# The low-weight blocks of a split fp32 weight tile at a pitch of 160 columns instead of 128

## The chip, the cores and the metric

The kernel runs on one core of one Trainium2 chip. Its time is the time on the device in microseconds (us), and the figure compared is the median over several executions. Engine names are those of the profile: PE is the matrix engine, PEld its weight loads (they overlap PE), DVE is VectorE, ACT is ScalarE, POOL is GpSimd, SP is the engine whose queue issues most DMAs.

## The reference

Two layers of a bidirectional hybrid encoder over 272 rows (16 learned meta tokens and 256 tokens) of width 2048, in float32:

```
proj = h @ w_in                              # 2048 x 6176
y_gla = gla_mixer(q, k, v, r, low-rank decay)
y_na  = na_mixer(q, k, v, rel_bias)
h  = layer_norm(ALPHA * h + concat(y_gla, y_na) @ w_out)
ff = square(relu(h @ w_ff1)) @ w_ff2         # 2048 -> 8192 -> 2048
h  = layer_norm(ALPHA * h + ff)
```

The meta tokens are dropped from the output. Nearly all the arithmetic is in the four products with `w_in`, `w_out`, `w_ff1` and `w_ff2`; the change touches how the weights of these products lie in the on-chip memory (SBUF), and nothing else.

## The kernel before, in words

**Split products.** A float32 weight `w` is split into a high part `wh` (the value rounded to the matrix engine's format `float32r`) and a low part `wl = w - wh`. Activations are split in the same way into a pair (high, low). A product is the sum of three: `wh` with the high activations, `wh` with the low ones, `wl` with the high ones.

**Weight tiles.** Weights stream from HBM in tiles of 128 partitions x 1024 columns (`WB`), 512 KB each, 768 of them in all, in the fixed order of `order` (line 150). `made` (line 172) issues a tile's DMA on SP's queue into `raw`, lets ACT copy it into `wh` (line 180) and DVE subtract into `wl` (line 181). `raw`, `wh` and `wl` come from the pool `wst` with three buffers for each name, so a new `wh` is written when the matmuls of the tile three places earlier have been done. `weights` (line 166) keeps two tiles made ahead. The very first tile goes through `head` (line 186), in quarters.

**Blocks.** Each tile holds eight blocks of 128 x 128, the stationary operands of eight matmuls. In `wh` and `wl` a block begins 128 columns (512 bytes) behind the one before it, so that all blocks begin at a multiple of 512 bytes from the tile's start.

**Three orders of matmuls.** `eight` (line 204), called by `by_m` (line 250), uses a tile for one output of 128 columns. In layer 0 (272 rows, now and then 274) it issues for each of eight blocks one matmul with the high and one with the low activations (line 216, 16 in all, high and low in turn), and then eight with `wl` and the high activations (line 219). In layer 1 most products need 256 rows alone; then high and low activations lie side by side, one matmul of 512 columns does both (line 213, eight in all), and eight of 256 columns with `wl` follow (line 219). `by_k` (line 230) uses a tile for four outputs in four PSUM banks: it issues its matmuls (line 246) in groups of four outputs, four with the high activations, four with the low ones, and so on, those with `wl` last.

**Activations.** A pair lies in one tile of two rows of 288 columns (`PITCH`, line 40): the low part of 272 columns begins 288 columns, that is 1152 bytes or 4.5 x 256, behind the high one. A `dense` pair of layer 1 (line 43) has its low part 256 columns, or 1024 bytes, behind the high one. `PAD` (line 39) is a dummy tile ahead of everything else that shifts where the later tiles begin. With a scratch area of 8192 bytes at the start of each partition, the tiles `x`, `y`, `u` of the activations, `raw`, `wh` and `wl` all begin at a multiple of 256 bytes.

The call that makes the program (line 1175) sets aside that scratch area (`dynamic_dma_scratch_size`).

Of the kernel before, what the change touches and what calls it, by code (L numbers as in the profile page):

```python
# [7 lines left out]
F32 = mybir.dt.float32  # L8
F32R = mybir.dt.float32r
U8 = mybir.dt.uint8  # L10
AF = mybir.ActivationFunctionType
ALU = mybir.AluOpType
PSUM = bass.MemoryType.PSUM

P = 128
# [11 lines left out]
WB = 1024  # L27
# [10 lines left out]
MEET = 2  # L38
PAD = 40
PITCH = 288  # L40


class Pair(tuple):
# [10 lines left out]
class Trunk:  # L54
# [117 lines left out]
    def made(self, ap, ends):  # L172
        if ap is None:
            return None
        nc = self.nc
        raw, wh, wl = (self.wp.tile([P, WB], d, name=nm, tag=nm)
                       for nm, d in (("raw", F32), ("wh", F32R), ("wl", F32R)))
        for c in map(slice, (0,) + ends, ends):
            nc.sync.dma_start(raw[:, c], ap[:, c])
            nc.scalar.copy(wh[:, c], raw[:, c])  # L180
            self.wl = nc.vector.tensor_tensor(wl[:, c], raw[:, c], wh[:, c].bitcast(F32), ALU.subtract).ins  # L181
        if not ends:
            self.head(ap, raw, wh, wl)
        return wh, wl

    def head(self, ap, raw, wh, wl):

        nc, q = self.nc, WB // 4
        both = self.xr.tile([P, 2, q + L], F32, name="head", tag="head", bufs=1)
        self.x[:2] = [self.pair(self.xp, "x", c) for c in range(2)]  # L190
        for c in range(2):
            nc.sync.dma_start(both[:, c], self.i["head"][:, c])
        nc.sync.dma_start(raw[:, 2 * q:], ap[:, 2 * q:])
        for c in range(2):
            at = slice(c * q, c * q + q)
            h, lo = (t[:, :L] for t in self.x[c])
            todo = [(both[:, c, q:], h, lo), (both[:, c, :q], wh[:, at], wl[:, at])]
            for args in todo[::-1] if c else todo:
                self.split(*args)
        for at in (slice(2 * q, 3 * q), slice(3 * q, WB)):  # L200
            nc.scalar.copy(wh[:, at], raw[:, at])
            self.wl = nc.vector.tensor_tensor(wl[:, at], raw[:, at], wh[:, at].bitcast(F32), ALU.subtract).ins

    def eight(self, ps, wh, wl, x, n, first, last, once):

        mm = self.nc.tensor.matmul
        c = lambda w, j: w[:, j * P:j * P + P]  # L210
        for j, v in enumerate(x):
            if once:
                mm(ps, lhsT=c(wh, j), rhs=v.once, start=first and not j, stop=False)  # L213
                continue
            for i in range(2):
                mm(ps[:, :n], lhsT=c(wh, j), rhs=v[i][:, :n], start=first and not i + j, stop=False)  # L216
        o = ps[:, T:] if once else ps[:, :n]
        for j, (h, _) in enumerate(x):
            mm(o, lhsT=c(wl, j), rhs=h[:, :T if once else n], start=False, stop=last and j == 7)  # L219
# [10 lines left out]
    def by_k(self, acts, n, before, wide=False):  # L230

        ps = [self.pm.tile([P, 512], F32, name="mm", tag="mm") for _ in range(4)]
        if wide:
            ps += [self.bank() for _ in range(4)]
        nk = len(acts)
        for k in range(0, nk, 2):
            before(k)
            for g in range(0, len(ps), 4):
                wh, wl = self.weights()
                parts = ((wh, 0), (wh, 1), (wl, 0))  # L240
                order = [(j, p, m) for j in range(2) for p in range(3) for m in range(4)]
                by_output = k == nk - 2 or k == 0 and not wide
                order.sort(key=lambda o: (o[0], o[2] // 2) if wide and not k + g else (by_output and o[2], o[1] // 2))
                for j, p, m in order:
                    c = j * 512 + m * P
                    self.nc.tensor.matmul(ps[g + m][:, :n], lhsT=parts[p][0][:, c:c + P], rhs=acts[k + j][parts[p][1]][:, :n],  # L246
                                          start=k + j + p == 0, stop=k == nk - 2 and j + p == 3)
        return [p[:, :n] for p in ps]

# [27 lines left out]
    def pair(self, pool, name, c):  # L277
        both = pool.tile([P, 2, PITCH], F32R, name=f"{name}{c}", tag=f"{name}{c}", bufs=1)
        return Pair(both, dense=name in ("y", "u") and not self.full)
# [94 lines left out]
    def load_gates(self):  # L374

        place = lambda c: self.yp.tile([P, 2, PITCH], F32, name=f"gw{c}", tag=f"y{c}", bufs=1).rearrange("p a c -> p (a c)")[:, :512]
        *self.wup, self.wlr = (place(c) for c in (8, 9, 10))
# [563 lines left out]
    def reuse(self, name, c, dtype):  # L941

        t = self.xp.tile([P, 2, PITCH], dtype, name=f"{name}{c}", tag=f"x{c}", bufs=1)
        return t.rearrange("p a c -> p (a c)")[:, :512]
# [235 lines left out]
```

## Time and profile before

| | |
|---|---|
| median of 3 executions | 2366.12 us (2366.05 to 2366.2) |
| the profiled execution | 2366.29 us |
| its span, first to last instruction | 2364.5 us |
| PE busy | 2356.2 us, 18180 matmuls |
| DVE busy | 1520.8 us |
| ACT busy | 1219.3 us |
| DMA | 419.02 MB, mean 177 GB/s |

A matmul's duration in the profile holds its latency, and matmuls overlap: some 287 ns for one of 272 columns, while the next one starts about 125 ns later. What the matrix engine needs for one is therefore read as the distance between starts, in the timeline: the start of a group of like matmuls, the start of the next group, and the count between them. The timeline rounds to 0.01 us, so that eight matmuls give a mean to about 1 ns and sixteen to about 0.6 ns. The line number behind an instruction names the source line, `out<-in` its tiles.

### The profile page before, as it was taken

The numbers are of one execution on the slowest core, as the hardware profiler recorded it, in microseconds if no ns is written. First come the engines' busy times: TensorE is split into PE (matmuls) and PEld (weight loads), VectorE is DVE, ScalarE is ACT, GpSimd is POOL, SyncE is SP. The second block draws the span as 40 slices with busy tenths as digits, with TensorE's granted clock in tenths as the row PEclk, the third lists the DMA queues.
The fourth block names the chain that finished last, engine by engine and source line by source line (L and its number), as shares of the span: only waits on it lengthen the run. The fifth ranks groups of instructions, "written<-read, shape, count | busy, mean of one in ns | idle before, by whom it ended". The sixth has DMA issues, their size and how long they took to land.

```text
span 2364.5 us, 44607 instructions
## 1 busy us (share of the span) xinstructions
PE 2356.2 (100%) x18180; PEld 2241.9 (95%) x18180; DVE 1520.8 (64%) x2432; ACT 1219.3 (52%) x2100; POOL 136.2 (6%) x200
## 2 busy tenths in 40 slices
PE   9999999999999999999999999999999999999998
PEld 9999999999999999999999899999988888888888
DVE  5588777775544455546576787778766455666654
ACT  5666664564433344444456666655644333444443
POOL 0021100100000000000030111101100000000000
PEclk9999999999999999999999999999999999999999
DMA  7454445555555555555555555455566666556664
GB/s 261 153 160 153 156 135 176 173 176 178 177 178 176 176 177 179 177 177 174 177 184 171 164 160 165 155 160 188 187 192 190 189 187 188 188 190 212 195 188 144
DMA packets 118301, 419.02 MB, mean 177 GB/s; under 512 B 13512, under 2 KB 14024, under 8 KB 118096
## 3 DMA queue, kind: packets, MB, share of 16 engines
q1 hardware_dynamic: 117808, 415.65, 55.8%
q8 instruction: 142, 2.33, 0.4%
q14 instruction: 63, 0.52, 0.1%
q10 hardware_dynamic: 288, 0.52, 0.1%
HBM read 414.03 MB, written 2.10 MB: 176 GB/s over the span
## 4 chain that ended last, share of the span: by engine, by line
PE 98%; DVE 1%; issue 0%; ACT 0%; POOL 0%; DVEq 0%; ACTq 0%; POOLq 0%
PE mm L216 35%; PE mm L219 29%; PE mm L213 22%; PE mm L246 6%; PE bg L246 1%; PE bg L757 1%; PE mm L696 1%; PE bg L557 0%; PE bg L403 0%; DVE wl L181 0%; PE mm L722 0%; PE mm L446 0%; PE bg L883 0%; PE bg L608 0%; PE bg L638 0%
## 5 line engine op out<-in xcount | busy, mean ns | idle before, releaser
L181 DVE TENSOR_TENSOR wl<-raw,wh 128x1024 fp32r<-128x1024 f32 (+1 forms) x768 | 941.8, 1227 | 621.5 <-ACT wh L180 618.4
L180 ACT CAST wh<-raw 128x1024 fp32r<-128x1024 f32 (+1 forms) x768 | 803.5, 1047 | 919.4 <-PE mm L216 367.7
L216 PE MATMUL mm<-x,wh 128*128 128x272 f32 (+2 forms) x4224 | 569.8, 287 | 0.0
L216 PEld LDWEIGHTS mm<-x,wh 128*128 128x128 f32 x4224 | 541.1, 188 | 0.8 <-PE mm L696 0.2
L219 PE MATMUL mm<-x,wl 128*128 128x272 f32 (+3 forms) x3264 | 466.9, 285 | 0.0
L219 PEld LDWEIGHTS mm<-x,wl 128*128 128x128 f32 x3264 | 437.5, 189 | 11.6
L213 PE MATMUL mm<-x,wh 128*128 128x512 f32 x1152 | 290.1, 394 | 0.0
L213 PEld LDWEIGHTS mm<-x,wh 128*128 128x128 f32 x1152 | 207.2, 189 | 37.9 <-PE mm L696 0.4
L219 PE MATMUL mm<-y,wl 128*128 128x272 f32 (+1 forms) x1408 | 200.5, 285 | 0.0
L219 PEld LDWEIGHTS mm<-y,wl 128*128 128x128 f32 x1408 | 189.5, 189 | 6.5
L216 PE MATMUL mm<-y,wh 128*128 128x272 f32 (+1 forms) x1440 | 193.3, 286 | 0.0
L216 PEld LDWEIGHTS mm<-y,wh 128*128 128x128 f32 x1440 | 184.3, 188 | 0.0
L213 PE MATMUL mm<-y,wh 128*128 128x512 f32 x688 | 172.6, 392 | 0.0
L219 PE MATMUL mm<-u,wl 128*128 128x272 f32 (+1 forms) x1024 | 145.8, 285 | 0.0
L213 PEld LDWEIGHTS mm<-y,wh 128*128 128x128 f32 x688 | 123.6, 189 | 21.9
L219 PEld LDWEIGHTS mm<-u,wl 128*128 128x128 f32 x1024 | 137.8, 189 | 4.8
L216 PE MATMUL mm<-u,wh 128*128 128x272 f32 (+1 forms) x1056 | 141.2, 286 | 0.0
L216 PEld LDWEIGHTS mm<-u,wh 128*128 128x128 f32 x1056 | 134.9, 188 | 0.0
L213 PE MATMUL mm<-u,wh 128*128 128x512 f32 x496 | 124.2, 392 | 0.0
L213 PEld LDWEIGHTS mm<-u,wh 128*128 128x128 f32 x496 | 89.2, 189 | 15.9
L246 PE MATMUL mm<-x,wh 128*128 128x272 f32 (+1 forms) x512 | 73.3, 288 | 0.0
L246 PEld LDWEIGHTS mm<-x,wh 128*128 128x128 f32 x512 | 67.9, 191 | 0.0
(273 smaller groups left out, 1856.5 us busy)
## 6 DMA issues: line engine op xcount, KB each, us to landing
raw<-in_wff SPq DMA_DIRECT2D x512, 512.0 KB, 3.6
raw<-in_win SPq DMA_DIRECT2D x190, 512.0 KB, 3.8
raw<-in_wout SPq DMA_DIRECT2D x64, 512.0 KB, 3.6
nb<-in_nab SPq DMA_DIRECT2D x16, 352.0 KB, 4.7
xraw<-in_xT SPq DMA_DIRECT2D x7, 272.0 KB, 5.2
out<-out SPq DMA_DIRECT2D x5, 256.0 KB, 3.2
brow<-in_norm SPq DMA_DIRECT2D x4, 256.0 KB, 4.8
gw<-in_wup SPq DMA_DIRECT2D x4, 196.0 KB
```

The costliest lines, as they stand in the source:

```text
L180: nc.scalar.copy(wh[:, c], raw[:, c])
L181: self.wl = nc.vector.tensor_tensor(wl[:, c], raw[:, c], wh[:, c].bitcast(F32), ALU.subtract).ins
L213: mm(ps, lhsT=c(wh, j), rhs=v.once, start=first and not j, stop=False)
L216: mm(ps[:, :n], lhsT=c(wh, j), rhs=v[i][:, :n], start=first and not i + j, stop=False)
L219: mm(o, lhsT=c(wl, j), rhs=h[:, :T if once else n], start=False, stop=last and j == 7)
L246: self.nc.tensor.matmul(ps[g + m][:, :n], lhsT=parts[p][0][:, c:c + P], rhs=acts[k + j][parts[p][1]][:, :n], start=k + j + p == 0, stop=k ...
L696: nc.tensor.matmul(ps[hh][:, t * NKEY:t * NKEY + NKEY], lhsT=q[hs, NM + t * P:NM + t * P + P], rhs=k[hs, t, :], start=True, stop=True)
L757: nc.tensor.matmul(po[t][hs, :P], lhsT=v2[ts, hs] if rest else v1[:, t, hs], rhs=p2[ts, hh, :] if rest else p1[:, 2 * hh + t, :], start=re ...
```

## The change

The high weights stay at a pitch of 128 columns. The low weights' tile grows from 1024 to 1280 columns (`SPAN`), and its blocks begin 128 + 32 (`SKEW`) columns, or 640 bytes, apart: block 0 at a multiple of 256 bytes, block 1 at 128 bytes past one, block 2 at a multiple again. `made`, `head` and the matmuls address blocks in place of columns; count, order, sizes and data of the copies, subtractions and matmuls stay. DVE now writes eight pieces of 128 columns with gaps of 32. The three buffers of `wl` take 3 x 1024 bytes more of each partition, and the scratch area shrinks from 8192 to 2048 bytes.

```diff
+SKEW = 32
+SPAN = 1280
...
-        raw, wh, wl = (self.wp.tile([P, WB], d, name=nm, tag=nm)
-                       for nm, d in (("raw", F32), ("wh", F32R), ("wl", F32R)))
+        raw = self.wp.tile([P, WB], F32, name="raw", tag="raw")
+        blocks = raw.rearrange("p (b c) -> p b c", c=P)
+        wh, wl = self.skewed("wh", 0, WB), self.skewed("wl", SKEW, SPAN)
         for c in map(slice, (0,) + ends, ends):
             nc.sync.dma_start(raw[:, c], ap[:, c])
-            nc.scalar.copy(wh[:, c], raw[:, c])
-            self.wl = nc.vector.tensor_tensor(wl[:, c], raw[:, c], wh[:, c].bitcast(F32), ALU.subtract).ins
+            self.halves(blocks, wh, wl, slice(c.start // P, c.stop // P))
...
+    def skewed(self, name, skew, size):
+        flat = self.wp.tile([P, size], F32R, name=name, tag=name)
+        return bass.AP(flat.tensor, flat.offset, [flat.ap[0], [P + skew, WB // P], [1, P]])
+
+    def halves(self, raw, wh, wl, at):
+        self.nc.scalar.copy(wh[:, at], raw[:, at])
+        self.wl = self.nc.vector.tensor_tensor(wl[:, at], raw[:, at], wh[:, at].bitcast(F32), ALU.subtract).ins
...
-        c = lambda w, j: w[:, j * P:j * P + P]
+        c = lambda w, j: w[:, j]
...
-                    c = j * 512 + m * P
-                    self.nc.tensor.matmul(ps[g + m][:, :n], lhsT=parts[p][0][:, c:c + P], rhs=acts[k + j][parts[p][1]][:, :n],
+                    self.nc.tensor.matmul(ps[g + m][:, :n], lhsT=parts[p][0][:, 4 * j + m], rhs=acts[k + j][parts[p][1]][:, :n],
...
-    nc = bacc.Bacc("TRN2", target_bir_lowering=False, num_devices=1, dynamic_dma_scratch_size=8192)
+    nc = bacc.Bacc("TRN2", target_bir_lowering=False, num_devices=1, dynamic_dma_scratch_size=2048)
```

More of the change, by code (lines that the diff above doesn't have):

```diff
@@ L175, in made, with head @@
         nc = self.nc
-        raw, wh, wl = (self.wp.tile([P, WB], d, name=nm, tag=nm)
-                       for nm, d in (("raw", F32), ("wh", F32R), ("wl", F32R)))
+        raw = self.wp.tile([P, WB], F32, name="raw", tag="raw")
+        blocks = raw.rearrange("p (b c) -> p b c", c=P)
+        wh, wl = self.skewed("wh", 0, WB), self.skewed("wl", SKEW, SPAN)
         for c in map(slice, (0,) + ends, ends):
             nc.sync.dma_start(raw[:, c], ap[:, c])
-            nc.scalar.copy(wh[:, c], raw[:, c])
-            self.wl = nc.vector.tensor_tensor(wl[:, c], raw[:, c], wh[:, c].bitcast(F32), ALU.subtract).ins
+            self.halves(blocks, wh, wl, slice(c.start // P, c.stop // P))
         if not ends:
-            self.head(ap, raw, wh, wl)
+            self.head(ap, raw, blocks, wh, wl)
         return wh, wl
-    def head(self, ap, raw, wh, wl):
+    def skewed(self, name, skew, size):
[4 more added lines that the diff above has]
+        self.wl = self.nc.vector.tensor_tensor(wl[:, at], raw[:, at], wh[:, at].bitcast(F32), ALU.subtract).ins
+    def head(self, ap, raw, blocks, wh, wl):
         nc, q = self.nc, WB // 4
@@ L194, in head @@
         for c in range(2):
-            at = slice(c * q, c * q + q)
+            at = slice(2 * c, 2 * c + 2)
             h, lo = (t[:, :L] for t in self.x[c])
-            todo = [(both[:, c, q:], h, lo), (both[:, c, :q], wh[:, at], wl[:, at])]
+            todo = [(both[:, c, q:], h, lo), (both[:, c, :q].rearrange("p (b c) -> p b c", c=P), wh[:, at], wl[:, at])]
             for args in todo[::-1] if c else todo:
                 self.split(*args)
-        for at in (slice(2 * q, 3 * q), slice(3 * q, WB)):
-            nc.scalar.copy(wh[:, at], raw[:, at])
-            self.wl = nc.vector.tensor_tensor(wl[:, at], raw[:, at], wh[:, at].bitcast(F32), ALU.subtract).ins
+        for at in (slice(4, 6), slice(6, 8)):
+            self.halves(blocks, wh, wl, at)
     def eight(self, ps, wh, wl, x, n, first, last, once):
         mm = self.nc.tensor.matmul
-        c = lambda w, j: w[:, j * P:j * P + P]
+        c = lambda w, j: w[:, j]
         for j, v in enumerate(x):
```

## The prediction

> **What bounds the kernel now.** I read the busy rows and the chain of waits first.
>
> ```profile
> span 2364.5 us, 44607 instructions
> PE 2356.2 (100%) x18180; PEld 2241.9 (95%) x18180; DVE 1520.8 (64%) x2432; ACT 1219.3 (52%) x2100; POOL 136.2 (6%) x200
> ...
> PE 98%; DVE 1%; issue 0%; ACT 0%; POOL 0%; DVEq 0%; ACTq 0%; POOLq 0%
> ```
>
> PE is busy all through, and 98% of the chain that ended last lies on it. So nothing but the distance between the starts of matmuls matters. I took it from the timeline of PE, first in layer 0:
>
> ```profile
> 601.21 2.14 PE L216 MATMUL mm<-x,wh 128*128 128x272 f32 x16
> 603.19 1.16 PE L219 MATMUL mm<-x,wl 128*128 128x272 f32 x8
> 604.19 2.14 PE L216 MATMUL mm<-x,wh 128*128 128x272 f32 x16
> ```
>
> The sixteen matmuls with high weights go from 601.21 to 603.19: 1.98/16 = 123.75 ns each. The eight with low weights go from 603.19 to 604.19: 1.00/8 = 125 ns each, although both have 272 columns. What differs: at line 216 the moving operand begins in turn at a multiple of 256 bytes (high activations) and 128 bytes past one (low), while the weights always begin at a multiple; at line 219 both always begin at a multiple. Narrow windows over the eight show where they lose it:
>
> ```profile
> 603.31 1.04 PE L219 MATMUL mm<-x,wl 128*128 128x272 f32 x7
> 603.45 0.91 PE L219 MATMUL mm<-x,wl 128*128 128x272 f32 x6
> 603.57 0.78 PE L219 MATMUL mm<-x,wl 128*128 128x272 f32 x5
> ```
>
> The steps from the group's start are 0.12, 0.14 and 0.12 us, then 0.62/5 = 0.124 us up to 604.19. The long step stands just where the turn of addresses stops. A second look at the same thing is `by_k` in layer 0, where the same kinds of weight and activation meet in another order, four high ones, then four low ones:
>
> ```profile
> 20.40 2.18 PE L246 MATMUL bg<-x,wh 128*128 128x272 f32 x16
> 22.41 1.17 PE L246 MATMUL bg<-x,wl 128*128 128x272 f32 x8
> 23.42 2.18 PE L246 MATMUL mm<-x,wh 128*128 128x272 f32 x16
> ```
>
> Here the sixteen take 2.01 us, 125.6 ns each, and the eight with low weights 1.01 us, 126 ns each. So sixteen high-weight matmuls of one shape cost 1.98 us where the address changes at each step and 2.01 us where it stays for four. `by_k` also changes the PSUM bank at each step, so the row alone doesn't prove that the address is the cause; that is why "no effect" stays a rival below. Then layer 1:
>
> ```profile
> 1899.97 1.12 PE L219 MATMUL mm<-u,wl 128*128 128x256 f32 x8
> 1900.08 1.00 PE L219 MATMUL mm<-u,wl 128*128 128x256 f32 x7
> 1900.92 2.00 PE L213 MATMUL mm<-u,wh 128*128 128x512 f32 x8
> 1902.08 0.84 PE L213 MATMUL mm<-u,wh 128*128 128x512 f32 x3
> 1902.76 1.12 PE L219 MATMUL mm<-u,wl 128*128 128x256 f32 x8
> ```
>
> The first low-weight matmul takes 0.11 us, the seven others 0.84/7 = 120 ns. Of the eight with 512 columns behind them, the first five take (1902.08 - 1900.92)/5 = 232 ns and the last three 0.68/3 = 227 ns: the change from one kind to the other leaves a trace for some five matmuls. The weight loads differ as well, in two windows of the grouped lines, 400 to 1200 us (layer 0) and 1600 to 2300 us (layer 1):
>
> ```profile
> L219 PEld LDWEIGHTS mm<-u,wl 128*128 128x128 f32 x496 | 66.0, 188 | 0.0
> ...
> L219 PEld LDWEIGHTS mm<-u,wl 128*128 128x128 f32 x432 | 58.9, 190 | 4.2
> ```
>
> A low-weight load takes 188 ns beside moving operands of 272 columns and 190 ns beside those of 256.
>
> **The change part by part.** What the skew can reach is counted by these rows, of the page and of the view by tile:
>
> ```profile
> L219 PE MATMUL mm<-x,wl 128*128 128x272 f32 (+3 forms) x3264 | 466.9, 285 | 0.0
> L219 PE MATMUL mm<-y,wl 128*128 128x272 f32 (+1 forms) x1408 | 200.5, 285 | 0.0
> L219 PE MATMUL mm<-u,wl 128*128 128x272 f32 (+1 forms) x1024 | 145.8, 285 | 0.0
> ...
> L246 PE MATMUL mm<-x,wl x256: 283/286/428, 5.5 to 1702.5; 128*128 128x272 f32 x96, 128*128 128x256 f32 x32
> L246 PE MATMUL mm<-y,wl x128: 279/284/296, 346.5 to 1564.9; 128*128 128x272 f32 x64, 128*128 128x256 f32 x64
> L246 PE MATMUL bg<-x,wl x64: 284/288/291, 10.3 to 53.4; 128*128 128x272 f32 x64
> ...
> L219 PE MATMUL mm<-x,wl 128*128 128x256 f32 x1152 | 160.4, 282 | 0.0
> L219 PE MATMUL mm<-y,wl 128*128 128x256 f32 x704 | 98.2, 282 | 0.0
> L219 PE MATMUL mm<-u,wl 128*128 128x256 f32 x512 | 71.4, 282 | 0.0
> ```
>
> In all 3264 + 1408 + 1024 + 256 + 128 + 64 = 6144 low-weight matmuls, eight for each of 768 tiles; 2368 of them are layer 1's of 256 columns at line 219. Every second one gets its weights from the other half of a 256-byte line.
>
> *Low weights in layer 0 (and `by_k`).* No row shows a weight load at a skewed address here. I take it that what counts is where weights and moving operand begin against each other; then a skewed weight against a straight activation is what a straight weight against a skewed activation is at line 216, and the low-weight group should run at that group's 123.75 ns instead of 125: -1.25 ns. From above it is bounded by nothing gained, and beyond that by the long step: 0.14 against 0.124 us, rounded about +10 ns, at each skewed block. From below by the 0.12 us of the first step: -5 ns.
>
> *Low weights in layer 1.* With 256 columns no row has addresses in turn. The nearest one is again layer 0's, so I take -1.25 ns, with the bounds 113 ns (the first of the group, 0.11 us, seven less than 120) and +10 ns as above.
>
> Together 6144 x 1.25 = 7.7 us less.
>
> *What it leaves behind.* The first five high-weight matmuls after a low-weight group in layer 1 take 232 - 227 = 5 ns more than the last three. There are 2368/8 = 296 such groups; if the new order left nothing behind this would give 296 x 5 x 5 = 7.4 us, if it left twice as much it would cost as much. No row says which: 0.
>
> *DVE's and ACT's share.* DVE writes eight pieces instead of one row; ACT reads and writes the same bytes. The nearest rows are a DVE operation of 272 elements with steps and one without:
>
> ```profile
> L543 DVE TENSOR_TENSOR S<-S,dec 128x272 f32<-128x272 f32 x64 | 27.1, 449 | 0.8 <-ACT U L534 0.5
> L801 DVE TENSOR_TENSOR ft<-ft 128x272 f32<-128x272 f32 x56 | 24.3, 436 | 0.3 <-ACT ft L800 0.3
> ...
> 639.95 2.14 PE L216 MATMUL mm<-y,wh 128*128 128x272 f32 x16
> 642.17 1.05 ACT L180 CAST wh<-raw 128x1024 fp32r<-128x1024 f32 x1 [1.90 <-PE mm L216]
> 643.25 1.23 DVE L181 TENSOR_TENSOR wl<-raw,wh 128x1024 fp32r<-128x1024 f32 x1 [1.72 <-ACT wh L180]
> ```
>
> 449 against 436 is 3%, or 37 ns of 1.23 us; below, nothing. It costs nothing: ACT's copy at 642.17 waited for line 216's matmuls begun at 639.95 to free a buffer, and this tile is used three tiles (of 604.19 - 601.21 = 2.98 us) later, its low part from 639.95 + 8.94 + 1.98 = 650.87. DVE is done at 644.48, over 6 us ahead. With that cover gone it would be 768 x 37 ns = 28 us.
>
> *Scratch area and later tiles.* The issues of DMAs are all by SP and ACT, on two queues beside those of instruction loading; no row shows POOL issuing one:
>
> ```profile
> q1 hardware_dynamic: 117808, 415.65, 55.8%
> q10 hardware_dynamic: 288, 0.52, 0.1%
> ...
> out<-out ACTq DMA_DIRECT2D x2, 256.0 KB, 2.6
> ```
>
> No wait is added, so I set the smaller scratch at 0. Tiles ahead of the low weights move down by 6144 bytes, those behind by 3072; both are multiples of 256, so no other operand changes its half.
>
> **Sum.** The profiled execution took 2366.29 us (its span and 1.8 us around it); 2366.29 - 7.7 = 2358.6. It lies 0.2 us above the median of the runs, so the forecast for the median is 2358.4 us, 0.33% less.
>
> **The rivals.** *No effect.* Order or PSUM bank, not the weights' address, makes 123.75, 125 and 125.6 ns different. For it: the steps of PE are uneven in every order. Then the time stays at 2366.1 +- 1.
>
> The Trainium skill speaks for this rival: "TensorE: Matmul & The Clock Gate", section "Step-by-step: what each phase is for", says that PE reads weights and moving operand through two independent ports, and that loading the next weights takes nothing from the running matmul; by it the sum would be 0. Its section "Back-to-back issue gap" gives N/2.4 + 2.5 ns for an undisturbed matmul, as an estimate 115.8 ns for 272 columns; the 125 ns above do not agree, so that something stalls each step which that page does not name.
>
> *A larger gain.* In layer 1 the weight load itself sets the 120 ns, being held up where it begins in the same half as the moving operand: loads take 190 ns there. If four of eight then take 113 ns, 296 x 4 x 7 = 8.3 us go, with the 7.4 us left behind also gone, and layer 0's and `by_k`'s share 3776 x 1.25 = 4.7: 2366.1 - 20.4 = 2345.7. Against it: the gain of 113 ns is seen once a group, right behind a matmul of 512 columns, which gives the load more time.
>
> *Slower.* In layer 1 the matmul is so short that the load has no slack, and a weight that begins in the other half than the one before makes a long step like that of layer 0, +10 ns, at each of 296 x 4 = 1184 skewed blocks: +11.8 us, less 4.7 in the rest: 2366.1 + 7.1 = 2373.2. It decides from 4.7/1184 = 4 ns a block. For it: the long step of layer 0 stands at a change in the addresses' order. Against it: at line 216 the order changes at every step and that is the fastest group. If layer 0 had the long steps too, with (6144 - 2368)/2 = 1888 skewed blocks, it would be 2366.1 + 11.8 + 18.9 = 2396.8.
>
> **How the numbers follow.** A measurement of this kernel can tell about 0.2% (4.7 us) from no change. The forecast, 2352 to 2362, gets 0.42; the larger gain 0.11; no effect 0.22; slower 0.25, of it 0.05 for long steps in both layers. Faster by over 0.2% (below 2361.4): 0.11 and most of 0.42, the rest of it lying within 0.2%: 0.50. Same 0.25, slower 0.25. The range leaves out the far ends of both sides: 2346 to 2378.
>
> **What would show it.** Right: the low-weight group at line 219 in layer 0 goes from 1.00 to 0.99 us or less, with no step of 0.14, in layer 1 from 0.95 to about 0.94, and line 216 stays at 1.98. The larger gain: in layer 1 0.93 or less and all eight matmuls of 512 columns near 227 ns. No effect: 1.00 and 0.95 stay. Slower: steps of 0.13 us or more at every second low-weight matmul. The forecast is wrong if line 213 or 216, whose operands don't move, changes by more than the low-weight groups, if PE waits for `wl`, or if line 181 takes over 1.5 us.

## The result, and the profile after

The changed kernel takes 2374.39 us (median of 7 executions, 2374.18 to 2375.0) against 2366.37 us before (7 executions beside it): 1.0034 times as long, 95% interval 1.0022 to 1.0046. It is slower by 8 us; 2358.4 us had been forecast.

The page of the changed kernel, busy rows and the chain of waits:

```profile
span 2373.1 us, 44607 instructions
PE 2365.0 (100%) x18180; PEld 2247.9 (95%) x18180; DVE 1520.3 (64%) x2432; ACT 1220.5 (51%) x2100; POOL 135.9 (6%) x200
...
PE 98%; DVE 1%; issue 0%; ACT 0%; POOL 0%; DVEq 0%; ACTq 0%; POOLq 0%
```

As many instructions as before, PE still on 98% of the chain, and the span 8.6 us longer. Line 225 is now the high-weight matmul of layer 0 (216 before), 222 that of layer 1 (213), 228 the low-weight one (219), 254 that of `by_k` (246). The timeline of PE in layer 0, and narrow windows over one low-weight group:

```profile
601.82 2.17 PE L225 MATMUL mm<-x,wh 128*128 128x272 f32 x16
603.82 1.16 PE L228 MATMUL mm<-x,wl 128*128 128x272 f32 x8
604.82 2.17 PE L225 MATMUL mm<-x,wh 128*128 128x272 f32 x16
606.83 1.16 PE L228 MATMUL mm<-x,wl 128*128 128x272 f32 x8
...
603.95 1.04 PE L228 MATMUL mm<-x,wl 128*128 128x272 f32 x7
604.07 0.91 PE L228 MATMUL mm<-x,wl 128*128 128x272 f32 x6
604.20 0.79 PE L228 MATMUL mm<-x,wl 128*128 128x272 f32 x5
...
605.83 1.16 PE L225 MATMUL mm<-x,wh 128*128 128x272 f32 x8
```

The low-weight group still takes 1.00 us. Its long step of 0.14 is gone, its steps are 0.13, 0.12, 0.13 and then 0.62/5, so that nothing is won. The sixteen high-weight matmuls, none of whose operands was moved to another half of its 256 bytes, take 2.00 and 2.01 us instead of 1.98. That isn't a bump at their start: their last eight, from 605.83 to 606.83, take 125 ns each, where the group before had 123.75. The starts of single matmuls, in nanoseconds, show two patterns. Before, the high-weight steps alternate between 126 and 121 ns in 329 of the 373 tiles of 272 columns that no other matmul interrupts; after, they do so in 22, and nearly all others run through four steps of about 125, 128, 124 and 123 ns.

The same in layer 1:

```profile
1900.88 1.11 PE L228 MATMUL mm<-u,wl 128*128 128x256 f32 x8
1901.82 1.99 PE L222 MATMUL mm<-y,wh 128*128 128x512 f32 x8
1903.65 1.10 PE L228 MATMUL mm<-y,wl 128*128 128x256 f32 x8
1904.59 2.03 PE L222 MATMUL mm<-y,wh 128*128 128x512 f32 x8
1906.45 1.11 PE L228 MATMUL mm<-y,wl 128*128 128x256 f32 x8
1907.40 1.76 PE L222 MATMUL mm<-u,wh 128*128 128x512 f32 x7
```

Here the low-weight group went from 0.95 to 0.94 or 0.95 us, and two kinds of tile take turns: 2.77 us (1901.82 to 1904.59) and 2.81 us (1904.59 to 1907.40), although both run the same instructions at addresses of the same halves. Summed over the whole trace, each matmul counted from its start to the start of the next:

| matmuls | before | after | change | forecast |
|---|---|---|---|---|
| high weights, 272 columns, 6016 | 747.8 us | 755.7 | +7.9 | 0 |
| high weights, 512 columns, 2336 | 539.1 | 540.9 | +1.8 | 0 |
| low weights, 272 columns, 3008 | 378.0 | 378.7 | +0.7 | -3.8 |
| low weights, 256 columns, 2368 | 283.0 | 280.4 | -2.7 | -3.0 |
| low weights in `by_k`, 448 | 55.7 | 56.1 | +0.4 | -0.6 |

These make +8.1 of the span's +8.6 us. The loss lies in the matmuls whose own operands the change left alone.

### The profile page after: what moved, and what is told of

It is laid out like the page before. It is cut to its first block, busy times and chain, and to the rows that moved or that the text cites. A ratio compares the mean times of both kernels' runs of the same rounds, so it can differ in the third digit from the quotient of the medians.

```text
span 2373.1 us, 44607 instructions
## 1 busy us (share of the span) xinstructions
PE 2365.0 (100%) x18180; PEld 2247.9 (95%) x18180; DVE 1520.3 (64%) x2432; ACT 1220.5 (51%) x2100; POOL 135.9 (6%) x200
## 4 chain that ended last, share of the span: by engine, by line
PE 98%; DVE 1%; issue 0%; ACT 0%; POOL 0%; DVEq 0%; ACTq 0%; POOLq 0%
PE mm L225 36%; PE mm L228 29%; PE mm L222 22%; PE mm L254 6%; PE bg L254 1%; PE bg L765 1%; PE mm L704 1%; PE bg L565 0%; PE bg L411 0%; DVE wl L194 0%; PE mm L730 0%; PE mm L454 0%; PE bg L891 0%; PE bg L616 0%; PE bg L646 0%
```

## The experiments

Three theories at first. **A**: what counts is where PE reads the low-weight blocks, and the state in which this leaves PE's two streams (weight loads and moving operand) is handed on to the high-weight matmuls behind. **B**: the other tiles' new places in SBUF do it. **C**: DVE's writes with gaps disturb PE's reads.

**All but the skew (e1_layout).**

```diff
-        wh, wl = self.skewed("wh", 0, WB), self.skewed("wl", SKEW, SPAN)
+        wh, wl = self.skewed("wh", 0, WB), self.skewed("wl", 0, SPAN)
```

> All of the change but the skew: the larger tile, the smaller scratch area, block-wise addressing, but low-weight blocks at a pitch of 128 columns again. Theory A (what counts is where the matrix engine reads the low-weight blocks, and the order in which their addresses alternate is handed on to the high-weight matmuls behind them): back to 2366.4 us within 1 us, sixteen high-weight matmuls of layer 0 in 1.98 us. Theory B (the other tiles' new places in SBUF are the cause): stays at 2374 us, sixteen in 2.00 to 2.01 us. Theory C (VectorE's writes with gaps disturb the matrix engine's reads): 2366.4 us, as A.

2366.52 us, 1.0001 of before (0.9991 to 1.001). Its timeline of layer 0:

```profile
702.68 2.14 PE L225 MATMUL mm<-u,wh 128*128 128x272 f32 x16
704.66 1.16 PE L228 MATMUL mm<-u,wl 128*128 128x272 f32 x8
705.66 2.14 PE L225 MATMUL mm<-u,wh 128*128 128x272 f32 x16
```

1.98 and 1.00 us, as before. B falls: the smaller scratch area, the larger tiles and the moved neighbours cost nothing.

**Skewed writes, straight or skewed reads (e2_even, e3_odd).**

```diff
-            mm(o, lhsT=c(wl, j), rhs=h[:, :T if once else n], ...
+            mm(o, lhsT=c(wl, j // 2 * 2), rhs=h[:, :T if once else n], ...      # e2_even
+            mm(o, lhsT=c(wl, j // 2 * 2 + 1), rhs=h[:, :T if once else n], ...  # e3_odd
```

> The changed kernel, low weights still written with gaps, but the low-weight matmuls read only the even blocks (0, 0, 2, 2, 4, 4, 6, 6), which all begin at a multiple of 256 bytes; the odd blocks' part of the products is left out. Theory A: 2366.4 us within 1.5, sixteen high-weight matmuls of layer 0 in 1.98 us. Theory B and theory C: 2374 us.

> As the run that reads even blocks, but only odd blocks (1, 1, 3, 3, 5, 5, 7, 7), all 128 bytes past a multiple of 256; the even blocks' part of the products is left out. Theory A: the relation to the straight activations is constant again, so the low-weight matmuls behave as with even blocks, 125 ns each in layer 0, but what they hand on can differ: between 2360 and 2376 us, and if the time differs from the even run's, at least half of the difference lies in the high-weight matmuls. Theories B and C: 2374 us.

2367.77 us with even blocks, 2377.21 us with odd ones. First the timeline of the even run, then of the odd one:

```profile
701.24 2.14 PE L225 MATMUL mm<-y,wh 128*128 128x272 f32 x16
703.22 1.16 PE L228 MATMUL mm<-y,wl 128*128 128x272 f32 x8
704.22 2.14 PE L225 MATMUL mm<-u,wh 128*128 128x272 f32 x16
```

```profile
702.71 2.17 PE L225 MATMUL mm<-y,wh 128*128 128x272 f32 x16
704.71 1.17 PE L228 MATMUL mm<-y,wl 128*128 128x272 f32 x8
705.72 2.15 PE L225 MATMUL mm<-u,wh 128*128 128x272 f32 x16
707.71 0.54 PE L228 MATMUL mm<-u,wl 128*128 128x272 f32 x3
```

DVE writes with gaps in both. With even blocks the steps are those of the kernel before (1.98 and 1.00), so C falls. It stands 1.5 us above the 2366.26 us of the kernel before beside it. By the starts of all matmuls these lie in `by_k`, which the edit leaves reading skewed blocks: 1.7 us more there, and every other group of matmuls that use weight tiles within 0.1 us. With odd blocks the high-weight group takes 2.00 and 1.99 us and the low-weight one 1.01. By the starts of all matmuls the odd run loses 5.8 us at line 225 and 0.9 at line 222 against the even one, 6.7 of the 9.4 us between the two. The low-weight matmuls of line 228 lose 4.6 us, where they had been expected to stay, and `by_k` takes 1.8 us less. Only the blocks that line 228 reads differ between these two kernels, so where the low weights are read sets the time, and most of the cost is paid by the others: that is theory A. Each of the two kernels ran once; the 17 executions of the kernel before beside them lie within 1.9 us.

**The skewed blocks first (e4_swap).**

```diff
-        for j, (h, _) in enumerate(x):
+        for i in range(8):
+            j = i ^ 1
```

> The changed kernel with all its parts, but the low-weight matmuls take the blocks in the order 1, 0, 3, 2, 5, 4, 7, 6: as many skewed blocks, the last one now a straight one. Theory A: the low-weight group itself stays within 0.01 us, and the high-weight matmuls behind it fall into another pattern: sixteen in layer 0 back at 1.98 us, the whole 2366 us or less. Theories B and C: 2374 us.

2372.38 us, 1.0025 of before (1.0015 to 1.0036). A row of each layer's two groups:

```profile
701.72 2.14 PE L225 MATMUL mm<-y,wh 128*128 128x272 f32 x16
703.70 1.17 PE L230 MATMUL mm<-y,wl 128*128 128x272 f32 x8
704.71 2.13 PE L225 MATMUL mm<-u,wh 128*128 128x272 f32 x16
...
1902.13 2.01 PE L222 MATMUL mm<-u,wh 128*128 128x512 f32 x8
1903.97 1.12 PE L230 MATMUL mm<-u,wl 128*128 128x256 f32 x8
1904.93 2.01 PE L222 MATMUL mm<-u,wh 128*128 128x512 f32 x8
```

Theory A had one of its two signs, and the whole stays over 6 us above what it gave. The order alone, with as many skewed blocks, puts layer 0's high-weight group back to 1.98 us, and against expectation layer 1 now takes longer: 2.80 us a tile (1902.13 to 1904.93), by the median of all tiles 2807 ns in place of 2793 before.

**All orders in two runs (e5_orders, e6_orders).** If order matters, all 70 orders of four straight (0) and four skewed (1) blocks can be read from one trace, eight tiles each:

```diff
+        k = (FROM + self.tiles[once] // 8) % len(ORDERS)
+        self.tiles[once] += 1
+        straight, skewed = [0, 2, 4, 6], [1, 3, 5, 7]
+        for i, odd in enumerate(ORDERS[k]):
+            j = (skewed if odd == "1" else straight).pop(0)
```

> A scan inside one run: the changed kernel, but each eight weight tiles take the low-weight blocks in another of the 70 possible orders of four straight (0) and four skewed (1) blocks, from the list's start (01010101, 10101010, 01010110, 01101010, 00001111 and on). All products are complete. Read from the starts of matmuls for each order apart. Theory A1 (the last low-weight load hands its address on): orders that end with 0 leave the sixteen high-weight matmuls of layer 0 at 1.98 us, orders that end with 1 at 2.00 to 2.01 us, whatever stands before. Theory A2 (the whole order sets a state of the two streams that is handed on, and settles into one of several patterns): orders with the same last address give different sums, 2.97 to 3.02 us a tile in layer 0. The whole run between 2362 and 2378 us by both.

> The same scan from the list's middle on, so that both layers see the remaining orders, and some orders come a second time at other tiles. Theory A1: as before, by the last address alone. Theory A2: an order seen in both scans gives the same sum within 2 ns, but orders with the same last address differ by 10 ns or more. The whole run between 2362 and 2378 us.

2374.06 and 2373.19 us as a whole. From the start of the high-weight group to the start of the next, median of the tiles that follow one of the same order, in ns:

```
order      layer 0        order      layer 1
10100110   2973           01101100   2753
10010101   2980           01100011   2760
01001101   2987           00011101   2767
10110010   3000           01100110   2793
01010101   3007           10101010   2806
10010110   3013           10110010   2824
10101001   3020           11010001   2827
all 0      2980           all 0      2793   (kernel before)
```

A1 falls: orders that end with 0 lie between 2973 and 3013 ns in layer 0, and those that end with 1 between 2976 and 3020; in layer 1 both kinds are among the shortest and the longest. A2 holds in that the whole order counts. Its second sentence held for some orders alone: in layer 0, 01001101 gave 2986 or 2987 ns in both scans, but 00110011 gave 2981 and 3020 in one scan and 2981 or 2982 and 3005 in turn in the other, so an order can run in more than one pattern. Straight blocks are nearly the best order for layer 0 and an average one for layer 1.

**The best orders throughout (e7_best).** From here on theory A2 means: the relation of the two streams' addresses sets a state, which settles into a pattern.

```diff
+LOW = (1, 0, 3, 2, 4, 5, 7, 6), (0, 1, 3, 2, 5, 7, 4, 6)
...
-        for j, (h, _) in enumerate(x):
-            mm(o, lhsT=c(wl, j), rhs=h[:, :T if once else n], start=False, stop=last and j == 7)
+        for i, j in enumerate(LOW[once]):
+            mm(o, lhsT=c(wl, j), rhs=x[j][0][:, :T if once else n], start=False, stop=last and i == 7)
```

> The changed kernel with the low-weight blocks in the orders that the scan found short: layer 0 takes 10100110 (blocks 1, 0, 3, 2, 4, 5, 7, 6), layer 1 takes 01101100 (blocks 0, 1, 3, 2, 5, 7, 4, 6). Theory A2 (the order of addresses sets a state that is handed on and settles): the sums of the scan hold when an order is kept throughout: 2973 ns a tile in layer 0 (7 less than the kernel before, 376 tiles) and 2753 in layer 1 (40 less, 296 tiles), so 2366.4 - 2.6 - 11.8 = 2352 us within 3. If the scan's sums were those of its mixed surroundings alone: 2362 to 2372 us.

2355.54 us, 0.9955 of before (0.9942 to 0.9969), a little over the range expected: faster than both kernels. The timeline, layer 0 and layer 1:

```profile
702.26 2.14 PE L226 MATMUL mm<-u,wh 128*128 128x272 f32 x16
704.24 1.16 PE L229 MATMUL mm<-u,wl 128*128 128x272 f32 x8
705.23 2.14 PE L226 MATMUL mm<-u,wh 128*128 128x272 f32 x16
...
1902.00 1.98 PE L223 MATMUL mm<-y,wh 128*128 128x512 f32 x8
1903.82 1.10 PE L229 MATMUL mm<-y,wl 128*128 128x256 f32 x8
1904.76 1.98 PE L223 MATMUL mm<-u,wh 128*128 128x512 f32 x8
1906.58 1.09 PE L229 MATMUL mm<-u,wl 128*128 128x256 f32 x8
```

Layer 1's tile is 2.76 us (1902.00 to 1904.76); its eight high-weight matmuls take 1.82 instead of 1.84 us and its low-weight ones 0.93 or 0.94 instead of 0.95. In layer 0 the low-weight group takes 0.99 us. Layer 0 gave less than the scan had promised: by the mean of all tiles 4 ns each instead of 7, since about one tile in seven ran in another pattern, of 2986 or 2987 ns.

**Relation or address (e8_all_up, e9_weights_up).** Both from the kernel before, with the scratch area of 2048 bytes to make room.

```diff
-PAD = 40
+PAD = 72                                            # e8_all_up
...
+        pool("gap", bufs=1).tile([P, 32], F32, name="gap", tag="gap")      # e9_weights_up
         self.wp = pool("wst", bufs=3)
+        pool("gap2", bufs=1).tile([P, 32], F32, name="gap2", tag="gap2")
```

> The kernel before with the dummy tile 32 columns longer (and the smaller scratch area, so that it fits): activations and weights all begin 128 bytes past a multiple of 256. If only the relation of the weights' address to the moving operand's counts: 2366.4 us within 1, the same steps as before in both layers. If the absolute half of the 256 bytes counts: another pattern, off by over 2 us either way.

> The kernel before with all weight tiles, high and low, 128 bytes past a multiple of 256 (a gap of 32 columns ahead of them, another behind), the activations where they were. If the relation counts: not the kernel before's steps; layer 1, where all loads and all moving operands keep one relation, gives the sum that one relation gives, up to 20 ns from 2793 ns a tile, and layer 0 changes its high-weight pattern, where high and low activations swap their parts. If the loads' addresses count for nothing beyond their change from block to block: 2366.4 us.

2365.63 us with everything moved by 128 bytes, 2379.94 us with the weights alone moved, one execution each; nine of the kernel before beside them lie between 2365.76 and 2367.18 us. The timelines, the first kernel and then the second:

```profile
701.87 2.14 PE L216 MATMUL mm<-u,wh 128*128 128x272 f32 x16
703.85 1.16 PE L219 MATMUL mm<-u,wl 128*128 128x272 f32 x8
704.85 2.14 PE L216 MATMUL mm<-u,wh 128*128 128x272 f32 x16
```

```profile
701.22 2.16 PE L218 MATMUL mm<-y,wh 128*128 128x272 f32 x16
703.22 1.18 PE L221 MATMUL mm<-y,wl 128*128 128x272 f32 x8
704.23 2.16 PE L218 MATMUL mm<-y,wh 128*128 128x272 f32 x16
...
1900.96 2.02 PE L215 MATMUL mm<-u,wh 128*128 128x512 f32 x8
1902.82 1.10 PE L221 MATMUL mm<-u,wl 128*128 128x256 f32 x8
1903.76 2.03 PE L215 MATMUL mm<-y,wh 128*128 128x512 f32 x8
```

With everything moved, 1.98 and 1.00 us stand as before. With the weights moved against the activations, the sixteen take 2.00 us and the tile of layer 1 that is shown 2.80 (1900.96 to 1903.76); over the whole trace, layer 1's tiles take 2799 or 2800 and 2820 or 2821 ns in turn. So it is the relation that counts, not the absolute half.

**A skew of 256 bytes (e10_skew64).** `SKEW = 64` and `SPAN = 1536`.

> The changed kernel with a skew of 64 columns: blocks 768 bytes apart, so that every one begins at a multiple of 256 bytes, while VectorE writes with larger gaps. If the 128-byte half is what counts: 2366.4 us within 1, with the steps of the kernel before. If any uneven pitch or gap does it: 2370 us or more.

2366.71 us in one execution, the steps of the kernel before (1.98 and 1.00 us in layer 0). So neither the uneven pitch nor the gaps cost anything by themselves; the shift by 128 bytes does. Shifts other than 128 and 256 bytes were not run.

**Layer 1 alone (e11_layer1, e12_layer1_best).**

```diff
-        wh, wl = self.skewed("wh", 0, WB), self.skewed("wl", SKEW, SPAN)
+        wh, wl = self.skewed("wh", 0, WB), self.skewed("wl", SKEW if self.l else 0, SPAN)
```

The second also takes layer 1's low-weight blocks in the order 0, 1, 3, 2, 5, 7, 4, 6.

> The skew for layer 1 alone, in plain order; layer 0's low-weight blocks are back at a pitch of 128. Theory A2: layer 0's sixteen high-weight matmuls are back at 1.98 us, so the loss of some 376 x 26 ns = 9.7 us goes; layer 1 keeps its two tile sums of 2814 and 2766 ns, 3 less a tile on average: 2366.4 - 0.9 = 2365.5 us within 1.5. If the loss were spread over both layers: about 2370 us.

> The skew for layer 1 alone, and there the order 01101100; layer 0 as in the kernel before. Theory A2: layer 1's 296 tiles at 2753 to 2755 ns in place of 2793, 2366.4 - 11.5 = 2354.9 us within 1.5, and nothing lost in layer 0, so no slower than the run with both layers reordered (2355.5). If part of the gain of that run came from layer 0: 2357 to 2359 us.

2365.84 us (0.9998, 0.9989 to 1.0007) and 2356.98 us (0.9961, 0.9948 to 0.9973). With the skew in layer 1 alone the loss is gone, as expected. With its best order as well the gain is 9.3 us, 2 us less than the 11.5 expected. By the starts, layer 1 gained 10.0 us and layer 0 lost 0.6: not all of layer 1's tiles gain 40 ns, and the 23 that have other matmuls in them or behind them gain nothing (2897.6 ns before, 2897.5 after). The run with both layers reordered is 1.4 us faster, against expectation, so that part of its gain, some 376 x 4 ns = 1.5 us, did come from layer 0.

## Why the prediction was wrong

**What bounds the kernel**: right. PE holds 96 to 99% of the chain that ended last in all of these runs.

**Low weights in layer 0 (and `by_k`)**: half of its assumption holds, that what counts is where weights and moving operand begin against each other (2365.63 us with both moved, 2379.94 with the weights alone). What I drew from it was wrong, that the group then runs at line 216's 123.75 ns. It stayed at 1.00 us; 3.8 us less was forecast and 0.7 us more measured. The row was one pattern of a whole sequence, and I had read it as the price of a single step.

**Low weights in layer 1**: right in size, -2.7 us where -3.0 was forecast, but by luck: the 1.25 ns came from a row of layer 0, where the mechanism behind it failed.

**What it leaves behind**: this is the step that failed, and it decided the sign. I saw that a low-weight group leaves a trace in the matmuls behind it, but bounded it for layer 1 alone, at its first five matmuls, and set it to 0. For layer 0 I gave it no term. There the trace of the new order doesn't fade: the high-weight group runs in a slower pattern to its end, 7.9 us in all, and with layer 1's 1.8 us the term set to 0 cost 9.7 of the 16 us between forecast and result. Most of the rest is the gain of the low weights that did not come. The even and odd runs show that the reads of the low weights cause it, and with the skew in layer 1 alone it is gone. The prediction had named this as a sign of being wrong: lines 213 and 216 changing by more than the low-weight groups.

**DVE's and ACT's share**: right. The subtraction's row by source line in the changed kernel:

```profile
L194 DVE TENSOR_TENSOR wl<-raw,wh x770: 416/1225/1476, 6.1 to 2351.8; 128x1024 fp32r<-128x1024 f32 x192, 128x256 fp32r<-128x256 f32 x1
```

Its median is 1225 ns with gaps in what it writes, 1226 before. **Scratch area and later tiles**: right, by the run without the skew.

**The rivals.** "No effect" falls with the 8 us of the result and with the even and odd runs: the address of the low weights does matter. The rule of the Trainium skill that spoke for it ("TensorE: Matmul & The Clock Gate", "Step-by-step: what each phase is for": weight loads take nothing from the running matmul) does not agree with 2365.63 us for all operands moved and 2379.94 us for the weights moved against the others; what the two streams have in common, these runs do not show. The prediction also read the section "Back-to-back issue gap" of that page too narrowly, as if it left no room for 125 ns against 115.8: there the Trainium skill says that the formula is for an isolated matmul, and that in a stream of weight loads and matmuls both set the spacing. "Slower" came near with 2373.2 us, but by coincidence: it put the loss on skewed blocks of layer 1, whose group became shorter. "A larger gain" was not this order's, but another order came near its signs in layer 1 (0.93 us for the eight low-weight matmuls, 227 ns for those of 512 columns): the best orders gave 0.93 or 0.94 us and 1.82/8 = 228 ns. It had asked for 20.4 us; 10.9 us came (2366.42 to 2355.54).

## What to carry to other kernels

In this kernel, where weight loads and matmuls run back to back, the step of a matmul is not a price of its own: it belongs to a pattern of the whole repeated sequence, and an edit to one group shows in the groups left alone. So where a kernel is like this, give every group that shares the stream a term with a bound on either side, and judge such a change by the sum over a whole period. When many orders are possible, put them all into one run, a few tiles each, read each one's period from the starts, and then run the best throughout: the scan promised 14 us here and 11 came.

## What the runs showed of the hardware that was not expected

The relation of the halves of 256 bytes between weight blocks and moving operand is worth from 2753 to 2827 ns for the same sixteen matmuls of layer 1, 2.7%, while PE waits for other engines for under 3 us of the whole run. Moving all operands by 128 bytes (2365.63 us) or widening the pitch by 256 (2366.71) changes the time by less than 1 us against 2366.42 us before.

The sums of a tile lie on a grid wherever an order has settled into a pattern that repeats with each tile: 2753, 2760, 2767, 2773, 2780, 2787, 2793, 2800, 2807, 2813, 2820 and 2827 ns in layer 1, and in layer 0 2973, 2980, 2987, 2993, 3000, 3007, 3013 and 3020. Values between belong to patterns that repeat only every second or third tile, and there the sum over the repeat lies on the grid: 2766 and 2814 in the changed kernel make 5580 ns, 837 steps of the grid. Of the 122 stretches of one order in the two scans that settle in this way, 121 fit within 0.5 ns, and the last, of 2797 ns a tile, does so over two tiles. The steps are 20/3 = 6.67 ns, as if the streams had to meet a fixed beat before a sequence can repeat. Why it is so, which part of PE or SBUF keeps that beat, and how an order leads to its pattern stays open: none of these runs tells.
